# A dilated convolution: the first image pair through another DMA queue, its cast on VectorE and ScalarE, two weight differences on GpSimd

## The chip, the cores and the metric

The kernel runs on one core of a Trainium2 chip. The metric is the time of one execution on the device, in microseconds (us). A core has five engines with instruction streams of their own: TensorE (PE in the profile; its weight loads are PEld), VectorE (DVE), ScalarE (ACT), GpSimd (POOL) and SyncE (SP). Transfers between the main memory and the on-chip memory are carried by 16 DMA engines, which all queues share: q1 holds what SyncE issues, q0 what GpSimd issues. GpSimd's DMAs can convert the type on the way; the others copy.

## What is computed

A 3 x 3 convolution with dilation 2 and a padding of 2, over 16 images of 64 channels and 64 x 64 pixels, into 128 channels, in f32. Cut to its core, the reference is

```python
x_pad = np.pad(x, ((0, 0), (0, 0), (2, 2), (2, 2)))
for kh in range(3):
    for kw in range(3):
        output[b, co] += weight[co, ci, kh, kw] * x_pad[b, ci, kh*2:kh*2+64, kw*2:kw*2+64]
```

The input is 16.8 MB, the output 33.5 MB.

## The kernel before

**Fewer products.** Rows come in groups of four: two rows with e = 0 and the two below with e = 1, so that row h + 2 is the row with the other e. With s = x0 + x1 (the sum of the two kinds of rows of one group), both outputs of a group share the middle product: y0 = w1 s + (w2 - w1) x1 + w0 x1 of the group above, and y1 = w1 s + (w0 - w1) x0 + w2 x0 of the group below. That is five products with a row of the kernel in the place of six. The five weight sets w0, w1, w2, w21 (w2 - w1) and w01 (w0 - w1) are made once.

**Tiles.** Two images make a pair: their 2 x 64 channels fill the 128 partitions. A pair is kept as `x16` (f16, 4096 elements for each partition, 6 buffers), its sums as `s16` (3 buffers), the output of a pair as `o` (f32, two images of 4096 elements, 32 KB for each partition, 3 buffers). There are 8 pairs, and each is worked in 4 units of 16 rows (`u`).

**A unit** has three phases on TensorE, each into a PSUM tile `ps` of two banks (one for each image of the pair), of which there are four. The first phase is w1 with s16 (6 matmuls); ScalarE copies it to `s32` (line 189). The second and third are the rows of e = 0 and of e = 1 (12 matmuls each), and VectorE adds s32 to each and writes `o` (line 194). After two units (first and last pair) or four (the others) SyncE sends the finished rows out, one DMA for each image (line 205).

**Loads.** The function `load` (line 69) issues from GpSimd a DMA that reads f32 and writes f16. Pair 0 is loaded in two parts, rows 0 to 35 and 36 to 63, pair 1 in one, right at the start (lines 76 and 77); pairs 2 to 4 after GpSimd's first sum (line 133), pairs 5 to 7 later, in the loop (line 181). The function `prepare` (line 121) makes the sums on GpSimd: pair 0 in four parts, cut at rows 20, 36 and 52, the others in two.

**The start.** SyncE loads the weights (line 63). VectorE writes zeros, six matmuls without use run on them (line 87). GpSimd makes an identity matrix (line 83). When the weights have landed, ScalarE converts all nine taps to f16, twice, once for each image of a pair (line 93), and VectorE makes the differences w21 and w01, twice each (line 96). TensorE turns the five sets in the order w1, w21, w0, w01, w2, three matmuls for each (line 107), and VectorE (the first, third and fifth set) and ScalarE (the second and fourth) bring them from PSUM to `w_sb` (lines 116 and 118). The first phase of pair 0 needs the first part of its sums and the set w1.

**Order.** The schedule is written by hand: each engine runs its instructions in the order of the program text, and so does each queue of DMAs. An instruction that waits holds all that stand behind it on its engine. GpSimd issues its DMAs itself, between its other instructions. The waits are put in by the framework from the tiles that are read and written.

Of the kernel before, what the change touches and what calls it, by code (L numbers as in the profile page):

```python
# [10 lines left out]
def kernel(  # L11
# [7 lines left out]
    nc = tc.nc  # L19

    B, CI, H, W = x.shape
# [5 lines left out]
    P = 128  # L27
    f32 = mybir.dt.float32
    f16 = mybir.dt.float16
# [20 lines left out]
    x16pool = ctx.enter_context(tc.tile_pool(name="x16pool", bufs=6))  # L50
    sumpool = ctx.enter_context(tc.tile_pool(name="sumpool", bufs=3))
    spool = ctx.enter_context(tc.tile_pool(name="spool", bufs=2))
    opool = ctx.enter_context(tc.tile_pool(name="opool", bufs=3))
# [5 lines left out]
    x_pair = x.rearrange("(nb two) c h w -> nb (two c) h w", two=2)  # L59
# [5 lines left out]
    x16 = {}  # L65
    s16 = {}


    def load(pb, cuts):
        x16[pb] = x16pool.tile([P, H, W], f16, tag="x16", name=f"x16_{pb}")  # L70
        for lo, hi in zip(cuts, cuts[1:]):
            nc.gpsimd.dma_start(out=x16[pb][:, lo:hi], in_=x_pair[pb, :, lo:hi])  # L72

    cuts0 = [0, 20, 36, 52, H]
    AHEAD = 5
    load(0, [0, 36, H])
    load(1, [0, H])


    zero = wpool.tile([P, NB], f16, name="zero")  # L80
# [12 lines left out]
        nc.scalar.copy(out=w16[:, 0:NK, u, :], in_=w32k)  # L93
    for name, a in (("w21", 2), ("w01", 0)):
        for u in range(2):
            nc.vector.tensor_sub(  # L96
                out=w16[:, SLOT[name] * KW : (SLOT[name] + 1) * KW, u, :],
                in0=w32k[:, a * KW : (a + 1) * KW, :],
                in1=w32k[:, KW : 2 * KW, :],
            )  # L100

    w_sb = wpool.tile([P, NS * KW, CO], f16, name="w_sb")
    for n, name in enumerate(("w1", "w21", "w0", "w01", "w2")):
        ps = cpool.tile([P, 2, NB], f32, tag="ps", name=f"wt{n}")
        k0 = SLOT[name] * KW
        for j in range(KW):
            nc.tensor.matmul(  # L107
                out=ps[:, 0, j * CO : (j + 1) * CO],
                lhsT=w16[:, k0 + j, :, :].rearrange("o t i -> o (t i)"),
                rhs=ident,  # L110
                start=True,
                stop=True,
            )
        dst = w_sb[:, k0 : k0 + KW, :].rearrange("p k o -> p (k o)")
        if n % 2 == 0:
            nc.vector.tensor_copy(out=dst, in_=ps[:, 0, 0 : KW * CO])  # L116
        else:
            nc.scalar.copy(out=dst, in_=ps[:, 0, 0 : KW * CO])  # L118


    def prepare(pb, lo, hi):
        if pb not in s16:
            s16[pb] = sumpool.tile([P, 2 * NQ, W], f16, tag="s16", name=f"s16_{pb}")
        src = x16[pb].rearrange("p (q e r) w -> p q e (r w)", e=2, r=2)
        dst = s16[pb].rearrange("p (q r) w -> p q (r w)", r=2)
        q0, q1 = lo // 4, hi // 4
        nc.gpsimd.tensor_add(  # L127
            out=dst[:, q0:q1], in0=src[:, q0:q1, 0, :], in1=src[:, q0:q1, 1, :]
        )

    prepare(0, 0, 20)
    for pb in range(2, AHEAD):
        load(pb, [0, H])
    for lo, hi in zip(cuts0[1:], cuts0[2:]):
        prepare(0, lo, hi)
# [39 lines left out]
    for pb in range(NP):  # L175
        o = opool.tile([P, 2, H, W], f32, tag="o", name=f"o{pb}")
        ov = o.rearrange("p b (q e r) w -> p b q e (r w)", e=2, r=2)
        for u in range(NU):

            if u == 1 and AHEAD <= pb + 2 < NP:  # L180
                load(pb + 2, [0, H])
            if pb + 1 < NP:
                if u == 1:
                    prepare(pb + 1, 0, 36)
                elif u == 2:
                    prepare(pb + 1, 36, H)

            s32 = spool.tile([P, 2, NB], f32, tag="s32", name="s32")
            nc.scalar.copy(out=s32, in_=phase(pb, u, [("w1", 2, 0)]))  # L189
            for e, terms in enumerate(  # L190
                ([("w21", 1, 0), ("w0", 1, -1)], [("w01", 0, 0), ("w2", 0, 1)])
            ):
                ps = phase(pb, u, terms)
                nc.vector.tensor_add(  # L194
                    out=ov[:, :, u * UQ : (u + 1) * UQ, e, :],
                    in0=ps.rearrange("p b (q c) -> p b q c", c=QW),
                    in1=s32.rearrange("p b (q c) -> p b q c", c=QW),
                )


            step = NU // 2 if pb in (0, NP - 1) else NU
            if (u + 1) % step == 0:
                fl = slice((u + 1 - step) * 4 * UQ, (u + 1) * 4 * UQ)
                for hb in range(2):
                    nc.sync.dma_start(out=out[2 * pb + hb, :, fl], in_=o[:, hb, fl])
# [35 lines left out]
```

## Time and profile before

| what | value |
|---|---|
| median of 3 runs | 127.37 us (127.33 to 127.8) |
| the profiled execution | 127.64 us |
| its span, first to last event on the core | 125.9 us |
| TensorE busy | 106.6 us (85%) |
| VectorE busy | 80.7 us (64%) |
| ScalarE busy | 37.0 us (29%) |
| GpSimd busy | 39.6 us (31%) |
| read from and written to the main memory | 17.07 MB and 33.55 MB |

In the profile, a group of instructions is named by its line, engine and operation, with the tiles written and read; its busy time is a sum over all of them. The row of slices cuts the span into 40 equal pieces of 3.1 us and shows a busy share in tenths. A window row gives, for one stretch of the span, the busy time of PE, PEld, DVE, ACT and POOL with the number of instructions in brackets, then the granted clock of TensorE, the mean busy share of the DMA engines (it can be a little over 1 where packets overlap) and the GB/s that they moved. A load that converts f32 to f16 is counted there by the f16 that it writes, half of what it reads.

### The profile page before, as it was taken

The numbers are of one execution on the slowest core, as the hardware profiler recorded it, in microseconds if no ns is written. First come the engines' busy times: TensorE is split into PE (matmuls) and PEld (weight loads), VectorE is DVE, ScalarE is ACT, GpSimd is POOL, SyncE is SP. The second block draws the span as 40 slices with busy tenths as digits, with TensorE's granted clock in tenths as the row PEclk, the third lists the DMA queues.
The fourth block names the chain that finished last, engine by engine and source line by source line (L and its number), as shares of the span: only waits on it lengthen the run. The fifth ranks groups of instructions, "written<-read, shape, count | busy, mean of one in ns | idle before, by whom it ended". The sixth has DMA issues, their size and how long they took to land.

```text
span 125.9 us, 2253 instructions
## 1 busy us (share of the span) xinstructions
PE 106.6 (85%) x981; PEld 54.7 (43%) x981; DVE 80.7 (64%) x72; ACT 37.0 (29%) x37; POOL 39.6 (31%) x33
## 2 busy tenths in 40 slices
PE   6348999999999999999999999999999999950000
PEld 2143455555555555555555555555555555520000
DVE  0550367787778777877778778777877787770000
ACT  4733033333333333333333333333333333310000
POOL 6139797868077008600840093000000000000000
PEclk9999999999999999999999999999999999997555
DMA  4899999999999999999999999999999999999981
GB/s 107 143 215 223 213 211 216 234 281 294 401 292 284 383 297 323 328 427 312 312 325 419 427 432 432 437 417 417 437 427 458 417 409 417 437 411 427 427 349 47
DMA packets 4329, 42.37 MB, mean 337 GB/s; under 512 B 480, under 2 KB 480, under 8 KB 864
## 3 DMA queue, kind: packets, MB, share of 16 engines
q1 hardware_dynamic: 3024, 33.85, 63.8%
q0 software_dynamic: 1296, 8.39, 32.9%
q8 instruction: 7, 0.11, 0.3%
q14 instruction: 2, 0.02, 0.0%
HBM read 17.07 MB, written 33.55 MB: 402 GB/s over the span
## 4 chain that ended last, share of the span: by engine, by line
PE 80%; DMA 6%; POOL 1%; DVE 1%; DVEq 1%; issue 1%; POOLq 0%
PE ps L172 80%; DMA x<-in_x_dram 6%; POOL s L127 1%; DVE o L194 1%; DVEq L236 1%; DVEq L194 0%; POOLq L222 0%
## 5 line engine op out<-in xcount | busy, mean ns | idle before, releaser
L194 DVE TENSOR_TENSOR o<-ps,s 128x1024 f32<-128x1024 f32 x64 | 77.0, 1223 | 27.9 <-PE ps L172 26.2
L172 PE MATMUL ps<-x,w_sb 64*128 64x496 f16 (+3 forms) x768 | 86.6, 372 | 0.0
L172 PEld LDWEIGHTS <-w_sb 64*128 64x128 f16 x960 | 52.5, 96 | 51.5 <-issue 5.2
L189 ACT COPY s<-ps 128x1024 f32<-128x1024 f32 x32 | 32.4, 1012 | 70.3 <-PE ps L172 70.3
L127 POOL TENSOR_TENSOR s<-x 128x1152 f16<-128x1152 f16 (+4 forms) x18 | 34.0, 1911 | 36.1 <-PE ps L172 27.8
L172 PE MATMUL ps<-s,w_sb 64*128 64x496 f16 (+1 forms) x192 | 26.5, 379 | 2.1 <-POOL s L127 2.1
L72 POOL DMA_DIRECT2D x<-in_x_dram x9 | 5.1, 570 | 0.8 <-POOLq L222 0.8
L87 PE MATMUL warm<-zero 128*128 128x512 f16 x6 | 2.7, 627 | 1.2 <-DVE zero L81 1.2
L107 PE MATMUL wt<-ident,w 128*128 128x128 f16 x15 | 1.8, 312 | 2.0 <-ACT w L93 2.0
L96 DVE TENSOR_TENSOR w<-w 128x192 f16<-128x192 f32 x4 | 1.7, 495 | 2.5 <-DMA w<-in_weight_dram 2.5
L107 PEld LDWEIGHTS <-w 128*128 128x128 f16 x15 | 1.5, 145 | 2.9 <-ACT w L93 2.9
L93 ACT CAST w<-w 128x576 f16<-128x576 f32 x2 | 2.3, 1212 | 1.6 <-DMA w<-in_weight_dram 1.6
L116 DVE CAST w_sb<-wt 128x384 f16<-128x384 f32 x3 | 1.7, 557 | 1.4 <-PE wt L107 1.2
L87 PEld LDWEIGHTS <-zero 128*128 128x128 f16 x6 | 0.7, 135 | 2.3 <-DVE zero L81 1.2
L93 ACT ACT_TABLE_LOAD x1 | 1.3, 1283 | 0.7 <-PEq L222 0.7
L118 ACT CAST w_sb<-wt 128x384 f16<-128x384 f32 x2 | 1.0, 479 | 1.1 <-PE wt L107 1.1
L81 DVE MEMSET zero<- 128x256 uint32 x1 | 0.3, 272 | 0.9 <-PEq L222 0.9
masks.py:199 POOL TENSOR_SCALAR_AFFINE_SELECT ident<-ident 128x128 f16<-128x128 f16 x1 | 0.3, 295 | 0.1
masks.py:197 POOL MEMSET ident<- 128x128 f16 x1 | 0.2, 233 | 0.0
L222 POOL MEMSET const-float32-0.0<- 128x1 f32 x1 | 0.1, 100 | 0.2 <-issue 0.2
L222 POOL MEMSET const-bfloat16-1.0<- 128x1 bf16 x1 | 0.1, 103 | 0.0
L222 POOL MEMSET const-uint8-127<- 128x1 uint8 x1 | 0.1, 103 | 0.0
(1 smaller groups left out, 0.1 us busy)
## 6 DMA issues: line engine op xcount, KB each, us to landing
out_dram<-o SPq DMA_DIRECT2D x12, 2048.0 KB, 16.8
out_dram<-o SPq DMA_DIRECT2D x8, 1024.0 KB, 12.3
x<-in_x_dram POOLq DMA_DIRECT2D x7, 1024.0 KB, 15.5
x<-in_x_dram POOLq DMA_DIRECT2D x1, 576.0 KB, 7.1
x<-in_x_dram POOLq DMA_DIRECT2D x1, 448.0 KB, 8.6
w<-in_weight_dram SPq DMA_DIRECT2D x1, 288.0 KB, 2.8
```

The costliest lines, as they stand in the source:

```text
L72: nc.gpsimd.dma_start(out=x16[pb][:, lo:hi], in_=x_pair[pb, :, lo:hi])
L87: nc.tensor.matmul(out=warm[:, 0], lhsT=zero[:, 0:P], rhs=zero, start=True, stop=True)
L93: nc.scalar.copy(out=w16[:, 0:NK, u, :], in_=w32k)
L96: nc.vector.tensor_sub(out=w16[:, SLOT[name] * KW : (SLOT[name] + 1) * KW, u, :], in0=w32k[:, a * KW : (a + 1) * KW, :], in1=w32k[:, KW : ...
L107: nc.tensor.matmul(out=ps[:, 0, j * CO : (j + 1) * CO], lhsT=w16[:, k0 + j, :, :].rearrange("o t i -> o (t i)"), rhs=ident, start=True, st ...
L116: nc.vector.tensor_copy(out=dst, in_=ps[:, 0, 0 : KW * CO])
L118: nc.scalar.copy(out=dst, in_=ps[:, 0, 0 : KW * CO])
L127: nc.gpsimd.tensor_add(out=dst[:, q0:q1], in0=src[:, q0:q1, 0, :], in1=src[:, q0:q1, 1, :])
L172: nc.tensor.matmul(**m)
L189: nc.scalar.copy(out=s32, in_=phase(pb, u, [("w1", 2, 0)]))
L194: nc.vector.tensor_add(out=ov[:, :, u * UQ : (u + 1) * UQ, e, :], in0=ps.rearrange("p b (q c) -> p b q c", c=QW), in1=s32.rearrange("p b ( ...
L236: with _tile.TileContext(nc) as tc:
```

## The change

Pair 0 gets an f32 tile `x32`, which lies in one of the three buffers of `o`. SyncE loads it, unconverted, in two parts, right behind the weights. The f16 tile of pair 0 is written by VectorE (rows 0 to 19, after the copy of the first weight set) and by ScalarE (rows 20 to 35, 36 to 51 and 52 to 63, after its last copy of a weight set). GpSimd's sums of pair 0 read x32. The two instructions for w01 move from VectorE to GpSimd, and the load of pair 1 moves behind the first of them. The loads of pairs 2 to 7 keep their places in the text.

```diff
+    cuts0 = [0, 20, 36, 52, H]
+    x32 = opool.tile([P, 2, H, W], f32, tag="o", name="x32")[:, 0]
+    x16[0] = x16pool.tile([P, H, W], f16, tag="x16", name="x16_0")
+    for lo, hi in ((0, 36), (36, H)):
+        nc.sync.dma_start(out=x32[:, lo:hi], in_=x_pair[0, :, lo:hi])
...
-    cuts0 = [0, 20, 36, 52, H]
     AHEAD = 5
-    load(0, [0, 36, H])
-    load(1, [0, H])
...
     for name, a in (("w21", 2), ("w01", 0)):
         for u in range(2):
-            nc.vector.tensor_sub(
+            eng = nc.vector if name == "w21" else nc.gpsimd
+            eng.tensor_sub(
                 out=w16[:, SLOT[name] * KW : (SLOT[name] + 1) * KW, u, :],
                 in0=w32k[:, a * KW : (a + 1) * KW, :],
                 in1=w32k[:, KW : 2 * KW, :],
             )
+            if name == "w01" and u == 0:
+                load(1, [0, H])
...
             nc.scalar.copy(out=dst, in_=ps[:, 0, 0 : KW * CO])
+        if n == 0:
+            nc.vector.tensor_copy(out=x16[0][:, 0:20], in_=x32[:, 0:20])
+    for lo, hi in zip(cuts0[1:], cuts0[2:]):
+        nc.scalar.copy(out=x16[0][:, lo:hi], in_=x32[:, lo:hi])
...
-        src = x16[pb].rearrange("p (q e r) w -> p q e (r w)", e=2, r=2)
+        src = (x16[pb] if pb else x32).rearrange("p (q e r) w -> p q e (r w)", e=2, r=2)
```

## The prediction

> **What bounds the kernel now.** I read the page's second part first: PE is busy from slice 3 on, and so is the DMA row. Two things can set the end then, and the chain of waits names only the first of them.
>
> ```profile
> 9.84 100.97 PE ps L172 x948
> ```
>
> From the chain of waits, in order of time: start, duration, what. TensorE runs unbroken from 9.84 to 110.8 us. But the span is 125.9 us, and the chain ends at 113.3 (it follows instructions, not transfers). What fills the last 12 us is in the page's DMA parts.
>
> ```profile
> DMA  4899999999999999999999999999999999999981
> GB/s 107 143 215 223 213 211 216 234 281 294 401 292 284 383 297 323 328 427 312 312 325 419 427 432 432 437 417 417 437 427 458 417 409 417 437 411 427 427 349 47
> ...
> q1 hardware_dynamic: 3024, 33.85, 63.8%
> q0 software_dynamic: 1296, 8.39, 32.9%
> ```
>
> The DMA engines are busy from the second slice to the last but one: 63.8 + 32.9 = 96.7% of the span. The first slices' 215 GB/s are no slack: the cast loads are counted by their f16 side, and the read side is twice that, 430. So 16.8 MB of x read (41.4 us by the q0 row), 33.5 MB written and the weights keep 16 engines full. Windows late in the run settle it (columns: window, its length, five engines' busy time, granted clock, DMA share, GB/s):
>
> ```profile
> 66.00:112.00 46.00, 45.91 (x446) 23.63 (x441) 35.68 (x30) 15.19 (x15) 4.21 (x2) 1.00 1.00 426
> 112.12:125.90 13.78, 0.00 (x0) 0.00 (x0) 1.13 (x2) 0.00 (x0) 0.00 (x0) 0.60 0.75 315
> ```
>
> After VectorE's last result (112.12) 13.78 x 315 = 4.3 MB still leave; the last half pair is 2.1 MB of it. So 2.2 MB, at 426 GB/s some 5 us, were queued ahead of it. **The kernel is bound by its DMA engines**, with TensorE up to about 4 us ahead (I keep 1 us for the last issues, which start at 113.7). A microsecond comes only from DMA engines that start earlier, carry pair 0 in less time, or idle less; later, 10 to 122 us has share 1.01, so nothing is to be had there.
>
> Where they lose time is the start:
>
> ```profile
> 1.50:2.00 0.50, 0.50 (x2) 0.15 (x1) 0.00 (x0) 0.50 (x1) 0.50 (x2) 1.00 0.54 101
> 2.00:2.50 0.50, 0.50 (x3) 0.20 (x2) 0.00 (x0) 0.02 (x1) 0.50 (x2) 1.00 0.78 263
> 2.50:3.00 0.50, 0.50 (x3) 0.22 (x2) 0.00 (x0) 0.00 (x0) 0.50 (x2) 1.00 1.20 267
> 3.00:3.50 0.50, 0.50 (x3) 0.03 (x1) 0.00 (x0) 0.00 (x0) 0.42 (x2) 1.00 0.59 69
> 3.50:4.00 0.50, 0.43 (x2) 0.00 (x0) 0.41 (x1) 0.41 (x1) 0.06 (x1) 1.00 0.86 92
> 4.00:5.00 1.00, 0.00 (x0) 0.00 (x0) 1.00 (x4) 1.00 (x2) 0.00 (x0) 1.00 0.87 152
> 5.00:6.00 1.00, 0.03 (x1) 0.03 (x2) 0.32 (x1) 0.92 (x1) 0.00 (x0) 1.00 1.09 198
> 6.00:7.00 1.00, 1.00 (x10) 1.00 (x11) 0.49 (x1) 0.17 (x1) 0.00 (x0) 1.00 0.88 168
> 7.00:8.00 1.00, 0.75 (x8) 0.59 (x6) 0.83 (x3) 0.79 (x2) 0.00 (x0) 1.00 1.04 206
> 8.00:9.00 1.00, 0.00 (x0) 0.00 (x0) 0.35 (x1) 0.00 (x0) 0.60 (x1) 1.00 1.16 234
> ```
>
> The weights' 0.295 MB flow from about 1.75 (SyncE's issue at 0.74 plus 1.0). GpSimd's x follows, issued at 1.23, but thinly: 69, 92, 152 GB/s from 3 to 5 us where 215 is full.
>
> **The change, part by part.**
>
> *Pair 0's transfer.* Added up, these windows (and 0.05 MB before 2.0, which holds the first row) reach weights plus pair 0's f16 bytes, 0.295 + 1.049 = 1.344 MB, at 8.96 us: 1.119 MB by 8.0, and 0.225 MB at 234 GB/s. After the change SyncE issues x32 right behind the weights (0.74 + 0.37 = 1.11, a second at about 1.5), so its 2.097 MB follow in the same queue: start 1.75, weights 0.69 at 430 GB/s plus 0.25 for their slow first packets (267 instead of 430 for half a microsecond and more), and 2.097 MB. The trace has no f32 load of this size. Its nearest rows are the late stores (426) and the cast loads' read side (2 x 215 = 430); the weights' 263 (rows of 2.3 KB, at the start) is the slow bound. I take 420: 5.0 us, done at **7.7**. Gain 8.96 - 7.7 = **1.3 us**. At 263 GB/s it would be 8.0 us, done at 10.7, a loss of 1.7.
>
> The Trainium skill (DMA: Bandwidth & Descriptors, section SWDGE vs HWDGE vs iDMA, its table of a load stream) gives 408.7 GB/s for loads issued from SyncE; by it 5.1 us and a gain of 1.1. No row here shows that load yet.
>
> *The slowest DMA engine.* The mean is one end. The tail (188, 90, 16 GB/s in the microseconds from 122 to 125) says that the 16 engines end up to 3 us apart, and the last one sets the time. Pair 0's second part lands at 1.92 + 8.6 = 10.5 us, 1.5 after the mean; the weights land at 3.5, some 0.8 after theirs. If the late engines are late because of GpSimd's slow start, they gain 1.3 + 0.7 = 2.0. I take **1.4**, nearer the mean, since pair 1 still begins on GpSimd's queue.
>
> *Pair 1's load.* It moves from 2.44 to behind the mask, the weights' landing (3.59) and one subtraction on GpSimd. That operation is new there: 192 elements. GpSimd's adds take 923, 1178, 1390, 2366 ns for 384, 512, 640, 1152 elements: 1.88 ns each plus 0.2, so 0.56 us; f32 and a stride of nine could double or triple it, to 1.7. Issue at 4.2 (5.3), first bytes 1.5 later as in the first load (1.23 to about 2.7): 5.7 (6.8). The engines have pair 0 until 7.7: cover of 0.9 to 2 us. Without it each late microsecond costs one.
>
> *Loads of pairs 2 to 4* stand behind the second subtraction and pair 0's first sum (1.39 us for f16; with f32 inputs anything to 2.8). x32's first part lands at about 1.75 + 0.25 + 0.69 + 2.8 (1.18 MB) + 0.7 = 6.2 (the weights land 0.7 us after their mean end), so GpSimd's wait for x, 4.84 us before, ends 2 us sooner, and the loads are issued by 7.6 to 10; pair 1 keeps the engines until 12.7. Cost nothing.
>
> *VectorE* loses two subtractions (2 x 0.43 us) and gains a cast of 1280 elements: its 1024-element add takes 1.22, so 1.5 at most about 1.9 by the PSUM casts (557 ns for 384). Queued behind it are two copies of weights (to 9.7 us), wanted by the second and third phases. *ScalarE* gains casts of 1024, 1024 and 768 elements: by its 1.01 us copy 2.8 us, ahead of the first s32 copy, waiting for x32's second part. If that lands at 8.3, s32 is done at 11.8. Before, four PSUM tiles carried TensorE 6.6 us (9.84 to 16.42) without a release; starting at 7.6 to 9.0 it reaches that point at 14.2 or later. No stall. If pair 1's packets alternate with x32's (in 24 to 30 us two queues do share), the second part lands at about 13, s32 at 15.9, and TensorE stands for up to 1.7 us, still within the 4 us that it is ahead. Cost nothing. TensorE's first wait (2.09 us, for the first sum) shrinks, up to 2 us; next in line is the weights' first copy at 7.1. That gains nothing either, the DMA engines being last.
>
> *x32's slot* is the first of three for o; o2 waits for its readers, done by 15. Output tiles come round three pairs apart, as before. Nothing.
>
> **Sum.** Profiled execution 127.64 (span 125.9, 1.7 around it) - 1.4 = 126.2; the runs' median is 127.37, 0.27 lower: 127.37 - 1.4 = **126.0 us**. The measurement tells about 0.5%, 0.64 us, from no change.
>
> **Rivals.**
> - *Larger gain:* the slowest engine loses its whole late start: 2.0 or a little more, 125.3. For it: the uneven tail. Against: pair 1's first packets can be as uneven. 0.14.
> - *Only the issue is saved:* x32's packets pay the same slow start as the cast ones, which would then be the chip's first reads and not GpSimd's queue. Then only 1.23 - 1.11 = 0.1 us goes, with perhaps 0.2 for the cast: 127.1. For it: the weights' first packets are slow too. Against: 152 GB/s at 4 to 5 us is long after these. The Trainium skill has this as a rule (DMA: Bandwidth & Descriptors, Issuing engines are not separate DMA queues): starting DMAs on several engines saves only the issuing time. 0.14.
> - *The DMA engines run dry before pair 1 (slower):* place 7.7 us, price one for one. It undoes 1.4 when the first bytes come at 9.1, and shows as slower from 9.7, when GpSimd would have the subtraction done at 8.2, after 4.6 us instead of 0.56. 128.2 if they come at 10. For it: a shape that no row has. Against: 2.4 ns an element is the worst of four rows, 4.6 us is 24. 0.06.
> - *The front falls behind:* ScalarE's casts and GpSimd's f32 sums hold TensorE more than 4 us; needs x32's second part at 17 us. 128, 0.03.
> - Forecast: 0.63, its own range 125.6 to 126.7.
>
> Faster 0.63 + 0.14, less a little for small gains: 0.75; same 0.16; slower 0.09. Range: from the larger gain, 125.2, over the saved issue, to 127.3.
>
> **What would show it.** In the changed profile: about 400 GB/s from 3 to 7 us; no DMA share under 0.9 from 3 to 10; GpSimd's subtraction under 1.7 us; TensorE's first phase at 7.6 to 9.0; the share of 1.0 unbroken to about 120.5, and the same 5 us queue at VectorE's last result. It is wrong if f32 packets are slow, if share sinks near 8 us, or if TensorE's end moves the time.

## The result and the profile after

The changed kernel takes 126.79 us (median of 12 runs, 126.5 to 126.98), the kernel before 128.04 in the same set (127.0 to 128.9): ratio 0.991, 95% interval 0.988 to 0.994. Two more sets with the changed kernel gave 0.996 (0.992 to 0.9997) and 0.997 (0.9945 to 0.9994). So it is faster, by 0.3 to 0.9%, some 0.4 to 1.1 us; the forecast was 1.4 us. The largest of the three ratios belongs to the set whose kernel before was slowest (128.04, against 127.52 and 127.72 in the other two). The profiled execution took 126.65 us, its span 124.9 (before 127.64 and 125.9).

The DMA parts of the page after:

```profile
DMA  4999999999999999999999999999999999999990
GB/s 142 355 356 215 215 215 205 262 286 270 396 278 273 360 297 320 409 365 318 297 375 433 441 425 430 430 420 420 420 441 446 417 430 420 430 415 423 423 396 39
...
q1 hardware_dynamic: 3312, 35.95, 68.8%
q0 software_dynamic: 1008, 7.34, 28.5%
```

Pair 0 has gone from q0 to q1 and now counts by its f32 side: slices two and three show 355 where 143 and 215 stood. From the fourth slice on the rows look as before, and they end one microsecond sooner. TensorE, in the chain of waits, and two late windows:

```profile
9.25 55.26 PE ps L185 x516
```

```profile
66.00:112.00 46.00, 44.61 (x432) 24.40 (x428) 36.91 (x31) 14.17 (x14) 4.21 (x2) 1.00 1.01 427
...
110.84:124.90 14.06, 0.00 (x0) 0.00 (x0) 1.12 (x1) 0.00 (x0) 0.00 (x0) 0.67 0.77 326
```

TensorE starts 0.6 us sooner (9.25 for 9.84), and after VectorE's last result (110.84) 14.06 x 326 = 4.6 MB still leave. The bound has not moved: DMA share 1.01 from 66 to 112 us (1.00 before). What changed lies in the first 9 us:

```profile
1.50:2.00 0.50, 0.50 (x2) 0.15 (x1) 0.00 (x0) 0.50 (x1) 0.00 (x0) 1.00 0.62 83
2.00:2.50 0.50, 0.50 (x3) 0.20 (x2) 0.00 (x0) 0.02 (x1) 0.00 (x0) 1.00 0.71 240
2.50:3.00 0.50, 0.50 (x3) 0.23 (x2) 0.00 (x0) 0.00 (x0) 0.00 (x0) 1.00 1.31 475
3.00:3.50 0.50, 0.50 (x3) 0.03 (x1) 0.00 (x0) 0.00 (x0) 0.00 (x0) 1.00 1.07 290
3.50:4.00 0.50, 0.43 (x2) 0.00 (x0) 0.41 (x1) 0.41 (x1) 0.36 (x1) 1.00 0.96 313
4.00:5.00 1.00, 0.00 (x0) 0.00 (x0) 1.00 (x2) 1.00 (x2) 1.00 (x2) 1.00 1.00 369
5.00:6.00 1.00, 0.02 (x1) 0.02 (x2) 0.10 (x1) 0.93 (x1) 0.98 (x2) 1.00 0.97 409
6.00:7.00 1.00, 1.00 (x10) 1.00 (x11) 0.48 (x2) 0.16 (x1) 0.22 (x2) 1.00 0.94 377
7.00:8.00 1.00, 0.76 (x8) 0.59 (x6) 1.00 (x3) 0.84 (x3) 1.00 (x1) 1.00 1.04 437
8.00:9.00 1.00, 0.00 (x0) 0.00 (x0) 0.74 (x2) 0.90 (x1) 1.00 (x1) 1.00 1.15 289
```

The engines no longer starve from 3 to 5 us: 290, 313, 369 GB/s of f32, where before 69, 92, 152 of f16 stood, so 138, 184, 304 on the read side. These rows sum to 2.29 MB by 8.0, and weights and pair 0 are 2.39 MB: pair 0 is complete at about 8.3 us, not at 7.7 as predicted, and 8.96 before. Pair 1 follows without a gap (shares 1.04 and 1.15).

**A measure for the start.** For every run below I take the window from 0 to 20 us, turn its bytes into read-side bytes (a load with conversion counts twice; pair 0 only where it is loaded with conversion) and divide by 430 GB/s, the rate that all_f32 below shows for loads alone. What is missing from 20 us is the time that the DMA engines lost at the start. Before: 188 GB/s x 20 = 3.76 MB, of them 0.295 of weights, the rest twice, 7.22 MB, 16.8 us: 3.2 us lost. After: 249 x 20 = 4.98 MB, of them 2.392 MB of weights and f32, the rest twice, 7.57 MB, 17.6 us: 2.4 us lost. So 0.8 us of the span's 1.0 stand there. A store that moves before 20 us is counted twice by this, a small error. The experiments vary this loss.

### The profile page after: what moved, and what is told of

The parts are those of the page before. It is cut to its first block, busy times and chain, and to the rows that moved or that the text cites. A ratio compares the mean times of both kernels' runs of the same rounds, so it can differ in the third digit from the quotient of the medians.

```text
span 124.9 us, 2260 instructions
## 1 busy us (share of the span) xinstructions
PE 105.8 (85%) x981; PEld 56.6 (45%) x981; DVE 80.8 (65%) x71; ACT 39.6 (32%) x40; POOL 41.5 (33%) x33
## 3 DMA queue, kind: packets, MB, share of 16 engines
q0 software_dynamic: 1008, 7.34, 28.5%
## 4 chain that ended last, share of the span: by engine, by line
PE 79%; DMA 5%; DVE 2%; POOL 2%; DVEq 1%; issue 0%; SPq 0%
PE ps L185 79%; DMA x<-in_x_dram 5%; DVE o L207 2%; POOL s L140 2%; DVEq L249 1%; SPq L63 0%; DVEq L207 0%
## 5 line engine op out<-in xcount | busy, mean ns | idle before, releaser
L185 PEld LDWEIGHTS <-w_sb 64*128 64x128 f16 x960 | 54.3, 95 | 48.4 <-issue 3.7
L140 POOL TENSOR_TENSOR s<-x 128x1152 f16<-128x1152 f16 (+4 forms) x18 | 35.1, 1975 | 31.1 <-PE ps L185 27.7
L80 POOL DMA_DIRECT2D x<-in_x_dram x7 | 4.0, 579 | 0.0
L131 ACT CAST x<-x 128x1024 f16<-128x1024 f32 (+1 forms) x3 | 2.8, 974 | 0.8 <-DMA x<-in_x_dram 0.8
L102 POOL TENSOR_TENSOR w<-w 128x192 f16<-128x192 f32 x2 | 1.9, 952 | 2.3 <-DMA w<-in_weight_dram 2.3
L129 DVE CAST x<-x 128x1280 f16<-128x1280 f32 x1 | 0.8, 817 | 0.0
```

The source lines that it names most:

```text
L102: eng.tensor_sub(out=w16[:, SLOT[name] * KW : (SLOT[name] + 1) * KW, u, :], in0=w32k[:, a * KW : (a + 1) * KW, :], in1=w32k[:, KW : 2 * KW ...
L131: nc.scalar.copy(out=x16[0][:, lo:hi], in_=x32[:, lo:hi])
L140: nc.gpsimd.tensor_add(out=dst[:, q0:q1], in0=src[:, q0:q1, 0, :], in1=src[:, q0:q1, 1, :])
L185: nc.tensor.matmul(**m)
```

## The experiments

The theory: the 16 DMA engines set the end, and the gain is the time at the start in which they lie less idle, because SyncE's queue delivers pair 0 sooner than GpSimd's. Rivals: the gain is the conversion saved; the later load of pair 1 (or the moved differences) makes it; TensorE's earlier start makes it.

| run | ratio to before (95%) | profiled time, us | GB/s, 0 to 20 us | lost by 20 us | time less loss |
|---|---|---|---|---|---|
| before | | 127.64 | 188 | 3.2 | 124.4 |
| before_again | 1.001 (0.998 to 1.004) | 127.53 | 190 | 3.0 | 124.5 |
| after | 0.991 (0.988 to 0.994) | 126.65 | 249 | 2.4 | 124.3 |
| after_again | 0.996 (0.992 to 0.9997) | 127.91 | 242 | 3.1 | 124.9 |
| after_third | 0.997 (0.9945 to 0.9994) | 126.86 | 245 | 2.8 | 124.1 |
| pool_f32 | 1.005 (1.003 to 1.008) | 128.17 | 233 | 3.9 | 124.3 |
| pair1_late | 1.014 (1.010 to 1.018) | 129.10 | 219 | 5.2 | 123.9 |
| x_first | 1.030 (1.026 to 1.034) | 131.44 | 197 | 7.2 | 124.2 |
| pe_late | 0.9975 (0.995 to 1.0003) | 127.10 | 244 | 2.9 | 124.2 |
| pe_later | 1.016 (1.011 to 1.021) | 128.36 | 245 | 2.8 | 125.6 |
| subs_alone | 1.002 (0.998 to 1.005) | 127.71 | 188 | 3.2 | 124.5 |
| subs_back | 0.999 (0.996 to 1.002) | 128.61 | 246 | 2.7 | 125.9 |
| all_f32 | 1.001 (0.999 to 1.004) | 127.45 | 375 | 2.6 | 124.9 |

In nine of the thirteen profiles, over losses from 2.4 to 7.2 us, the time less the loss stays at 123.9 to 124.5; four lie higher and are taken up below. The two large losses carry this: among losses of 2.4 to 3.2 us the four exceptions (up to 1.6 us) are larger than the gain.

The same count can be carried on to 120 us, when every load has landed, by adding the f16 bytes of the converting loads once more (8.39 MB before, 7.34 MB after). Lost by then: before 4.5, before_again 4.4, after 3.7, after_again 4.1, after_third 3.8, pe_later 5.4, x_first 8.4 us. The time less this loss is 122.9 to 123.2 in ten of the thirteen profiles, pe_later among them, and 123.7 to 124.2 in after_again, subs_back and all_f32, whose transfers end more unevenly. From 20 to 120 us, before and before_again lose 1.3 to 1.4 us more and the three profiles of after 1.1 to 1.3. So TensorE's earlier start spares the DMA engines at most 0.3 us of idling there.

**pool_f32: the queue or the conversion.** Pair 0 unconverted, but by GpSimd:

```diff
-        nc.sync.dma_start(out=x32[:, lo:hi], in_=x_pair[0, :, lo:hi])
+        nc.gpsimd.dma_start(out=x32[:, lo:hi], in_=x_pair[0, :, lo:hi])
```

> Pair 0 still as f32 and with all of the casts, but issued by GpSimd (q0) in the place of SyncE (q1). Theory A, the gain comes from where pair 0's transfer starts: it is lost, first x bytes at 2.7 and thin until 5 us, pair 0 complete near 8.9 as before the change, ratio to before 0.997 to 1.003. Theory B, the gain comes from the conversion that the DMA engines no longer make: it is kept, pair 0 complete by 8.4, ratio about 0.991.

Windows from 0 to 9 us, of this run, of after and of before:

```profile
0.00:9.00 9.00, 4.52 (x21) 2.34 (x22) 2.76 (x5) 5.00 (x6) 4.74 (x12) 1.00 0.75 260
```

```profile
0.00:9.00 9.00, 4.52 (x21) 2.35 (x22) 4.01 (x7) 5.53 (x6) 5.26 (x10) 1.00 0.83 287
```

```profile
0.00:9.00 9.00, 4.52 (x21) 2.34 (x22) 3.67 (x8) 4.57 (x5) 3.06 (x10) 1.00 0.78 151
```

Read side by 9 us: 260 x 9 = 2.34 MB here. After: 2.58 MB plus the second half of 0.19 MB of pair 1, 2.77. Before: 1.36 MB, of which 1.06 counts twice, 2.42. So f32 through GpSimd's queue starts as slowly as the converted load did, and 0.43 MB or 1.0 us behind SyncE's. The other profiles agree: by 5 us, 0.77 to 0.91 MB (read side) have moved in the four runs in which GpSimd issues pair 0 (before, before_again, subs_alone, pool_f32), 0.93 to 1.07 MB in the nine in which SyncE does. So the earlier flow is the queue's; the conversion is worth nothing that shows. The first issues start only 0.08 us apart (1.25 and 1.17), and the second ones end 0.4 us apart (2.48 and 2.07), so the issuing alone does not make 1.0 us either. The ratio came out worse than expected, 1.005: with x32 late, GpSimd's sum ends at 10.8 and the loads of pairs 2 to 4 behind it start too late, so that share sinks to 0.90 and 0.95 from 11 to 16 us.

**pair1_late: idle engines cost one for one.** The load of pair 1 goes behind GpSimd's first sum:

```diff
-            if name == "w01" and u == 0:
-                load(1, [0, H])
...
-    for pb in range(2, AHEAD):
+    for pb in range(1, AHEAD):
```

> Pair 1's load stands behind GpSimd's first sum, with pairs 2 to 4. Theory A, the DMA engines set the end and idle time at the start costs one for one: x32 is complete at 8.3, pair 1's first bytes come at about 9.2 - 0.7 + 1.5 = 10.0, so DMA share is near zero for 1.7 us and the time rises by 1.7 us to 128.5, ratio to before 1.004. Theory B, the backlog at the end absorbs it: 126.8, ratio 0.991.

```profile
8.00:9.00 1.00, 0.67 (x6) 0.40 (x6) 1.00 (x1) 1.00 (x2) 1.00 (x2) 1.00 0.45 186
9.00:10.00 1.00, 1.00 (x8) 0.36 (x5) 1.00 (x3) 0.95 (x2) 1.00 (x3) 1.00 0.67 66
10.00:11.00 1.00, 1.00 (x8) 0.44 (x6) 0.01 (x1) 1.00 (x2) 1.00 (x3) 1.00 0.72 74
11.00:12.00 1.00, 1.00 (x10) 0.55 (x8) 0.00 (x0) 1.00 (x2) 1.00 (x1) 1.00 0.79 139
```

The median is 129.24, 2.45 above the changed kernel's 126.79 (of another set); more than the 1.7 expected, since pair 1 does not begin at full rate: 66, 74, 139 GB/s of f16 for three microseconds where 215 is full. The loss at the start rises by 2.8. TensorE's first phase begins *sooner* than in the changed kernel (8.45), and that helps nothing: later VectorE waits 5.9 us in one piece for a store to free its output tile, TensorE with it. This is the prediction's rival of the engines that run dry, made on purpose, and its price holds.

**x_first: which first transfer is slow.** The weights' DMA moves behind both DMAs of x32.

```diff
-    nc.sync.dma_start(out=w32, in_=weight.rearrange("o i h w -> o (i h w)"))
...
         nc.sync.dma_start(out=x32[:, lo:hi], in_=x_pair[0, :, lo:hi])
+    nc.sync.dma_start(out=w32, in_=weight.rearrange("o i h w -> o (i h w)"))
```

> On SyncE's queue pair 0 first, then the weights. x32 came at 290 to 370 GB/s from 3 to 5 us in the changed kernel, where 420 was expected. Theory A, every first transfer of the run is slow for its first 2 to 3 us whatever its shape: x32 is slow from 1.8 to 5 and the time stays near 126.8 (TensorE starts some 3 us later, which the DMA engines' lead covers). Theory B, the weights' small rows are what is slow: x32 runs at over 400 GB/s from 2.5 on, and 0.5 us or more is gained, 126.2. Theory C, TensorE's start counts: 129 to 130.

```profile
2.00:2.50 0.50, 0.50 (x3) 0.20 (x2) 0.00 (x0) 0.02 (x1) 0.00 (x0) 1.00 0.98 184
2.50:3.00 0.50, 0.50 (x3) 0.22 (x2) 0.00 (x0) 0.00 (x0) 0.00 (x0) 1.00 0.97 129
3.00:3.50 0.50, 0.50 (x3) 0.03 (x1) 0.00 (x0) 0.00 (x0) 0.00 (x0) 1.00 0.65 258
3.50:4.00 0.50, 0.44 (x2) 0.00 (x0) 0.00 (x0) 0.00 (x0) 0.00 (x0) 1.00 0.67 276
4.00:5.00 1.00, 0.00 (x0) 0.00 (x0) 0.00 (x0) 0.00 (x0) 0.00 (x0) 1.00 0.99 415
...
9.00:10.00 1.00, 0.00 (x0) 0.00 (x0) 0.58 (x2) 0.58 (x1) 0.53 (x1) 1.00 0.00 0
10.00:11.00 1.00, 0.00 (x0) 0.00 (x0) 0.94 (x1) 1.00 (x2) 1.00 (x2) 1.00 0.00 0
```

x32 in front is no faster: 129 to 276 GB/s until 4 us, then 415. So the first two to three microseconds are slow whichever of the two comes first, and the weights' small rows are not the cause (what is, no run here shows); my 420 GB/s from the first byte of x32 on could not be had. The time of 131 us has another reason, which the expectation overlooked: pair 1's load waits on GpSimd for the weights, which now land at 9.4, and the engines stand idle from 9 to 11 us and move 41 GB/s in the next. The time less the loss is 124.2, so this loss accounts for all of it and TensorE's late start (13.6) for nothing that shows; theory C gave the right time for the wrong reason.

**pe_late and pe_later: does TensorE's start count.** Matmuls without use, 12 and 28 of them, in front of the first phase:

```diff
+    warm2 = cpool.tile([P, 2, NB], f32, tag="ps", name="warm2")
+    for _ in range(12):
+        nc.tensor.matmul(out=warm2[:, 0], lhsT=zero[:, 0:P], rhs=zero, start=True, stop=True)
```

> Twelve matmuls without use between the turned weights and the first phase, 12 x 0.43 = 5.2 us from 7.8 on, so TensorE's first phase starts at 12.9 in the place of 9.25 and VectorE's last result comes up to 3.6 us later. Theory A, the DMA engines set the end and are some 4.7 us behind: the time stays at 126.8, ratio 0.991, and the DMA share stays at 1. Theory B, TensorE's chain sets the end: plus 3.6 us, 130.4, ratio 1.019.

TensorE's first phase starts at 12.13, 2.9 us later, and the median is 127.05, 0.1 to 0.3 above the changed kernel's three medians (126.79, 126.88, 126.96); its loss at the start, 2.9 us, lies among theirs (2.4 to 3.1), which may account for that. No changed kernel ran in its set; against the kernel before there, 127.23, the ratio of 0.9975 is not clear of no gain.

The delay was smaller than it looks. VectorE's last result comes only 0.6 us later (111.4), and most of the 2.9 us is made up in the first unit (after, then pe_late):

```profile
9.25 1.44 PE L185 MATMUL ps<-s,w_sb 64*128 64x512 f16 x6 [1.49 <-POOL s L140]
```

```profile
12.06 0.81 PE L189 MATMUL ps<-s,w_sb 64*128 64x512 f16 x6
```

Six matmuls of the first phase take 1.44 us in the changed kernel, where TensorE was idle before them, and 0.81 us behind the matmuls without use, though the rows give a granted clock of 1.00 to the first and of 0.50 to 8 to 11 us of the second; the cause is not shown. The second unit starts at 14.21 us in the changed kernel and at 15.08 in pe_late: TensorE is late by 0.9 us from there on, and that is all that pe_late tests. In the kernel before this unit starts at 15.75, so pe_late takes back about half of TensorE's gain of 1.5 us.

> Twenty-eight matmuls without use in front of the first phase, where twelve took 4.1 us (start of the first phase 12.1) and cost 0.3 us. At 0.3 us each the first phase starts at about 16.5, 7.2 us later than in the changed kernel. Theory A, the DMA engines set the end and are 4.7 us behind TensorE: 7.2 - 4.7 = 2.5 us come through, 129.3, ratio to the changed kernel 1.02. Theory B, they have no fixed lead and idle as soon as outputs come late: 7 us, 134.

The first phase starts at 14.71, 5.5 us later than in the changed kernel. The second unit starts at 17.67, 3.5 us later. The median is 129.65, 2.8 us above the changed kernel's in the same set; the profiled execution, at 128.36 the shortest of six, can show only a part of this. Here the lead is used up, but not where I had looked. Three windows of pe_later:

```profile
100.00:102.00 2.00, 2.00 (x24) 1.00 (x22) 1.53 (x2) 0.44 (x1) 0.00 (x0) 1.00 0.88 365
102.00:104.00 2.00, 2.00 (x24) 0.97 (x20) 1.57 (x2) 1.01 (x1) 0.00 (x0) 1.00 0.41 172
104.00:106.00 2.00, 2.00 (x24) 0.92 (x20) 1.69 (x2) 0.85 (x1) 0.00 (x0) 1.00 0.94 393
```

The queue empties at 102 to 104 us, before pair 6's output is issued at 102.86 (99.69 in the changed kernel, 3.2 us sooner). The idle shares, 0.12 and 0.59 of two windows, are 1.4 us; so at this place the engines had 3.2 - 1.4, about 1.8 us of work in hand, not the 4 us that the last output suggests. That 1.4 us is also why this run's last column is 125.6, and why the loss by 120 us, which holds it, brings the run in line.

**subs_alone and subs_back: the other parts of the change.** The first is the kernel before with only the differences and pair 1's load moved:

```diff
-    load(1, [0, H])
...
-            nc.vector.tensor_sub(
+            eng = nc.vector if name == "w21" else nc.gpsimd
+            eng.tensor_sub(
...
+            if name == "w01" and u == 0:
+                load(1, [0, H])
```

> The kernel before with the change's second part alone: the two differences for w01 on GpSimd and pair 1's load behind the first of them; pair 0 still converted by GpSimd's own load. Theory A, only pair 0's earlier flow gains: pair 0 keeps the engines until 9, pair 1's first bytes come at about 6, nothing runs dry, ratio to before 0.997 to 1.003. Theory B, pair 1 out of pair 0's way is a part of the gain: pair 0 lands earlier and the ratio is 0.995 or less.

The second is the changed kernel with both put back:

```diff
+    load(1, [0, H])
...
-            eng = nc.vector if name == "w21" else nc.gpsimd
-            eng.tensor_sub(
+            nc.vector.tensor_sub(
...
-            if name == "w01" and u == 0:
-                load(1, [0, H])
```

> The two differences for w01 are back on VectorE and pair 1's load stands first on GpSimd's queue; pair 0 as in the change. Theory A, only the flow of bytes at the start counts: the loads of two queues now share the engines from 2.7 us on, x32's second part lands later (13 us or so), but as many bytes are moved by 9 us, and the time is that of the changed kernel within 0.3 us. Theory B, moving pair 1 behind the weights is what makes pair 0 fast and so the kernel: TensorE starts 1 to 2 us later and the time goes back to 127.5 or more.

subs_alone is 1.002 of before: this part alone does nothing that shows. subs_back has a median of 127.21, 0.33 above the changed kernel on the same chip, with intervals that overlap, so whether it costs anything stays unclear. Against before it is 0.999, not clear of no gain either: each part by itself shows no gain, only both together do, and how they share it is open. Its loss at the start is 2.7, and x32's second part lands late, as expected: ScalarE's casts wait for it until 14.1 us (9.75 in the changed kernel). Its profiled execution, 128.61, ends unevenly (below) and is one of the two longest of twelve.

**all_f32: the conversion, for all pairs.** All loads unconverted into four tiles of 16 KB for each partition, ScalarE converting a quarter of the next pair in each unit:

```diff
-            nc.gpsimd.dma_start(out=x16[pb][:, lo:hi], in_=x_pair[pb, :, lo:hi])
...
+            eng.dma_start(out=x32s[pb][:, lo:hi], in_=x_pair[pb, :, lo:hi])
...
+    load(0, [0, 36, H], nc.sync)
+    load(1, [0, H], nc.sync)
+    load(2, [0, H], nc.sync)
+    load(3, [0, H], nc.sync)
...
+            if u == 0 and 1 <= pb and pb + 4 < NP:
+                load(pb + 4, [0, H], nc.scalar)
...
+            if pb + 1 < NP:
+                cast(pb + 1, 16 * u, 16 * (u + 1), nc.scalar)
```

> All eight pairs are loaded as f32 (pairs 0 to 3 by SyncE right behind the weights, 4 by GpSimd, 5 to 7 by ScalarE's queue), into four f32 tiles of their own, converted by ScalarE in four parts for each pair; GpSimd's sums read f32. Theory A, the DMA engines set the end: a packet that reads 16 KB takes 0.63 us with the conversion and 0.61 to 0.62 without, 2% of 14.7 MB or 34 us, so 0.4 to 0.9 us less, 126.0 to 126.4. Theory B, the casts and the slower sums hold TensorE, or loads come too late for the queue to stay full: 127.5 or more.

```profile
12.00:20.00 8.00, 8.00 (x78) 4.06 (x76) 6.03 (x6) 4.86 (x5) 5.92 (x4) 1.00 1.01 430
```

Here the engines do next to nothing but load f32 (the first store is issued at 18.4 us): 430 GB/s, twice the 215 of the converting loads (the slices of the page after). So the conversion costs the engines no time that shows, and there was nothing to gain; 127.45 is 0.5% above the changed kernel of the same set. TensorE was not what held it: VectorE's last result comes at 111.2 us, as in the changed kernel run beside it (111.4). The changed kernel stays the fastest of the versions run.

**after_again, after_third, before_again: the size of the gain.** The changed kernel twice more and the kernel before once more, unedited.

> The changed kernel itself, so that the others of this set stand beside it on one chip. 126.8 us, ratio to before 0.991 if before is at its earlier median of 128.0; with before at the 127.2 of the last set, 0.996.

> The changed kernel once more, for its size: two sets gave 0.991 and 0.996 against before, whose own runs spread from 126.9 to 129.2. Theory A, the gain is the 0.8 us that the engines have moved more by 9 us: ratio 0.992 to 0.996. Theory B, it is 1.2 us or more, since an uneven start of GpSimd's queue also costs at the end: 0.991 or less.

> The kernel before, for a second profile of its start and its tail. Theory A, its spread comes from how the 16 engines end, not from the bytes moved by 9 us: by 9 us the same amount as in the first profile within 0.2 us at full rate, and the tail after 122 differs with the time. Theory B, it comes from a start that is sometimes slower: the amount by 9 us differs as much as the time.

The loss at the start is 3.2 and 3.0 us in the two profiles of before, 2.4, 3.1 and 2.8 in the three of after: it varies from run to run by as much as the gain. The two profiles of before differ by 0.4 us at 9 us (151 and 161 GB/s, 2.42 and 2.60 MB on the read side), more than theory A allows, though their times are only 0.1 us apart; the cause of before's spread (126.9 to 129.4 over all sets) stays open. What a long execution of the changed kernel shows is its end. after_again's profile, 127.91 us:

```profile
123.00:124.00 1.00, 0.00 (x0) 0.00 (x0) 0.00 (x0) 0.00 (x0) 0.00 (x0) 0.50 0.06 25
124.00:125.00 1.00, 0.00 (x0) 0.00 (x0) 0.00 (x0) 0.00 (x0) 0.00 (x0) 0.50 0.04 16
```

A share of 0.06 is one of 16 engines, and 25 GB/s is about one engine's rate (430 / 16 = 27): this reads as one engine that works on for over a microsecond when the other 15 are done. subs_back shows the same two rows at 25 and 25, all_f32 one at 25. These are the three runs that stay high when the loss is counted up to 120 us. Why one engine lags in some executions was not settled.

## Why the prediction was right, point by point

- **The number** owes something to luck. 126.79 lies outside the forecast's own range (125.6 to 126.7), 0.3 us from the rival "only the issue is saved" (127.1), and inside the wide one. A gain of 1.25 us appears only against 128.04, the slowest of the sets of before; from the 127.37 that the sum started at it is 0.6 us, and 0.6 and 0.8 by the medians of the other two sets.
- **The bound** was right: the share of 1.0 and the queue behind VectorE's last result are still there, idle engines cost one for one (pair1_late, x_first), and from 20 to 120 us the engines lose nearly as much before as after, though TensorE starts sooner after. pe_late bears on this less than was meant, since TensorE was only 0.9 us late from its second unit on.
- **TensorE's lead of about 4 us** was wrong by half: read at the last output, where a backlog of two half pairs stands, it is 5 us; at pair 6's output it is 1.8 us, and that is where pe_later lost time. Every "cost nothing" of the sum rested on it; they held because TensorE started sooner, not later.
- **Pair 0 through SyncE, 1.3 us**, is the term that was mis-sized: pair 0 completes at 8.3 instead of 7.7, and the engines gain 0.8 us by 20 us (the two further profiles of after against before_again give less, 0.2 and nothing; by 120 us the three gain 0.3 to 0.8). About 420 GB/s came only from 5 us on (409, 377, 437); x32 came at 290 to 370 before, and no faster when it was first (x_first). The rival "only the issue is saved" had its reason half right, then: the slow start is in part that of the run's first transfers. The other part is GpSimd's queue, and pool_f32 shows it. So the rule quoted there from the Trainium skill (DMA: Bandwidth & Descriptors, Issuing engines are not separate DMA queues) did not hold at this start: 0.08 us between the starts of the issues, 0.4 between their ends, 1.0 us between the bytes. Its load rate, 408.7 GB/s, is also below the 430 measured here.
- **The slowest engine, 0.1 of a possible 0.7 us,** cannot be told from nothing: the tail after is as uneven (254, 82, 8 GB/s from 121 to 124 us, against 188, 90, 16 a microsecond later).
- **Pair 1's cover** held. GpSimd's difference took 1.11 us instead of 0.56 (bound 1.7), the load was issued at 4.69, and x32 kept the engines until 8.3.
- **VectorE and ScalarE** were off the path as expected, but the first sum was slower: 2.2 us with f32 inputs beside VectorE's cast, so TensorE started at 9.25, not by 9.0.

## What to carry to other kernels

Where the DMA row is full from the second slice on, work in idle time of the DMA engines: the bytes that they had not delivered by a fixed time, at the rate that they reach later, moved the end one for one here, and the kernel's chain of waits, 80% of it TensorE, had not shown it. It paid here to put the first large load behind the smallest necessary one on SyncE's queue, and to let a GpSimd load begin under its cover. Read an engine's lead at every output, not at the last one: the smallest counts.

## What the runs showed of the hardware

VectorE's cast of f32 (1280 elements) and GpSimd's sum (640) hold each other up, whichever begins later. In the changed kernel's profile they start together and the cast is served first (GpSimd, then VectorE):

```profile
6.99 2.22 POOL L140 TENSOR_TENSOR s<-x 128x640 f16<-128x640 f32 x1 [0.78 <-DMA x<-in_x_dram]
```

```profile
7.00 0.82 DVE L129 CAST x<-x 128x1280 f16<-128x1280 f32 x1
```

In after_again GpSimd is 0.2 us ahead:

```profile
6.90 1.54 POOL L140 TENSOR_TENSOR s<-x 128x640 f16<-128x640 f32 x1 [0.56 <-DMA x<-in_x_dram]
```

```profile
7.13 1.99 DVE L129 CAST x<-x 128x1280 f16<-128x1280 f32 x1
```

The one that is ahead takes 0.82 or 1.54 us, and the other ends 1.4 or 0.7 us behind it: both are done within 2.2 us. The Trainium skill says this (SBUF — State Buffer, SBUF: two separate sides) of GpSimd's operations and of some of VectorE's, those in a two-port mode among them: the two engines share a pair of ports as a lock, held by whichever starts first for its whole instruction. The rows agree, as far as two starts 0.01 us apart can be put in order. In a profile, the duration of such an instruction is then partly a wait that no row of waits names.

TensorE's granted clock was 0.50 from 8 to 11 us in pe_late, and 0.83 on average over the first 20 us in before_again, after_third, subs_alone and subs_back, 1.00 in the other profiles of before and after; the times do not follow it, as is to be expected where the DMA engines set the end.
